# w_in weights as float16 pairs in a hybrid attention and mLSTM layer: one conversion form for all four pieces instead of two forms in turn

## The chip, the cores and the metric

The kernel runs on one core of a Trainium2 chip. The metric is the device time of one execution in microseconds (us). An engine works through its own list of instructions in order and waits for others by semaphores: PE (TensorE) multiplies matrices, ACT (ScalarE) and DVE (VectorE) work element by element, POOL (GpSimd) does a smaller part of that, SP issues most of the transfers between memory (HBM) and the on-chip buffer (SBUF). Products land in PSUM, a small buffer of banks which ACT and DVE read out.

## The reference

One layer of a diffusion backbone over 128 context tokens and 1024 latent tokens, with attention heads and mLSTM heads side by side. Cut to what touches the change:

```python
h = rmsnorm(x, norm1_w) * (1 + sc1) + sh1
aq, ak, av, mq, mk, mv, mo, mg = jnp.split(h @ w_in, SPLIT_POINTS, axis=-1)
...
attn_o = attention(aq, keys, vals)
hm, st_f, st_b = mlstm_bidir(heads(mq), heads(mk) * (MLSTM_DK ** -0.5), heads(mv), gates, init_f, init_b)
hm = rmsnorm(hm...) * jax.nn.sigmoid(mo)
mix = jnp.concatenate([attn_o, hm], axis=-1) @ w_out
x = x + g1 * mix
h2 = rmsnorm(x, norm2_w) * (1 + sc2) + sh2
x = x + g2 * swiglu(h2, w_gu, w_down)
```

D_MODEL is 1024. Of the 2832 columns of w_in, 512 make the queries aq, 256 the keys and values of attention, 16 the gates, and each of the four mLSTM heads has 4 x 128 columns (its mq, mk, mv and mo). The layer norm, the attention, the scans, w_out and the SwiGLU behind them are not changed.

## The kernel before

The 1152 tokens stand as nine blocks of 128 (block 0 is the context, 1 to 8 the latent tokens), in three groups of three. All matrices are float32, and a product with w_in is made from pairs: a weight is scaled by a power of two and split into a float16 "hi" and the float16 rest "lo", the activations h likewise (`hTh`, `hTl`), and three matmuls add hi*hi, hi*lo and lo*hi in PSUM.

The class `Scaled` (from L179) does this for a set of columns of w_in. A set is four pieces `raw` of 128x1024 float32 (1024 rows of w_in are 8 x 128, a piece holds two of the eight and 512 columns). `ready()` takes four `iraw` buffers, loads them (L193), finds the largest absolute value by two ACT passes for each piece (L198) and forms the scale; `pairs()` (L211) makes each piece a pair in an `ipair` buffer; `inverses()` forms the factors that undo the scale. There are four `iraw` and four `ipair` buffers in all. So the load of the next set's piece waits until the pair of the old piece is made (its DVE pass reads `raw` last), and the pair of a next piece waits until PE has used the old pair for the last time.

In the kernel before, `pairs()` has two forms in turn. Pieces 0 and 2 (the even form): ACT multiplies by the scale and rounds to float16 (L218), DVE computes raw*scale - hi (L219). Pieces 1 and 3 (the odd form): ACT multiplies `raw` by the scale in place (L221), ACT copies the result to float16 (L222), DVE subtracts (L137, the line of the helper `sub`). L221 needs only the piece and the scale; L218 and L222 also need the free `ipair` buffer.

Six sets go through it. `kvg` (keys, values, gates) comes first, with 128x544 pieces, and asked for the even form for all four, by `kvg.pairs(1)` at L378. Then come `w_q`, the attention queries (L971), head 0 (L978), and heads 1 to 3 in `head_project` (L746). For the last five sets half of the pieces have the odd form: ten even and ten odd pieces.

In the phase of the heads, `head_project(h)` first computes the transposed queries of all nine blocks, with the pairs as the moving side (`q_group`, L808 to L810), then block after block, 0 to 8, the k, v and o columns (`linear_tok`, L483 to L485); `evac` reads each block's PSUM bank out: `kt` (L755), `va` (L757) and `th` (L760), the last of which frees the bank. Two banks, named `wi`, serve these products. `evac` then transposes kt on PE (L116), copies it (`kT`, L767) and updates the state (L783, L785, `cs` L792 or L796). At the end of a head stands the turn to the next set: PE finishes block 8 with the old pairs, ACT and DVE convert the next set, and PE's next `q_group` needs both a free `wi` bank and the new pairs. Woven in between are the scans of the head before (`head_mlstm`: `dt` L849, `it` L869, `hm` L886, `jkh` L889) and the attention of the blocks: scores S in the only buffer of that name (L1035), their maximum (L1037), the exponential `pr` (L1038, which frees S), and the pair `ph` (L1041) and `pl` (L1042).

The order of each engine's list is not that of the source: a scheduler places the instructions by priorities and by a simulated time of its own for each of them. So a change of one instruction's kind can move the others around it.

Of the kernel before, what the change touches and what calls it, by code (L numbers as in the profile page):

```python
# [13 lines left out]
AF = mybir.ActivationFunctionType  # L14
ALU = mybir.AluOpType
# [30 lines left out]
def hybrid_step(ctx: ExitStack, tc: tile.TileContext, I: dict, O: dict):  # L46
    nc = tc.nc
    mm = nc.tensor.matmul
    act = nc.scalar.activation
    dve = nc.vector  # L50
# [7 lines left out]
    def nm(s):  # L58
        uid[0] += 1
        return f"{s}_{uid[0]}"  # L60
# [10 lines left out]
    def emit(gen):  # L71
        for _ in gen:
            pass
# [62 lines left out]
    def sub(out, full, hi, eng):  # L136
        (dve if eng == "dve" else pool).tensor_tensor(out=out, in0=full, in1=hi, op=ALU.subtract)  # L137
# [41 lines left out]
    class Scaled:  # L179
# [28 lines left out]
            dve.tensor_scalar(out=t[:, 10:11], in0=t[:, 8:9], scalar1=0.5, scalar2=None, op0=ALU.mult)  # L208
            self.inv, self.inv_k, self.inv_half = t[:, 8:9], t[:, 9:10], t[:, 10:11]

        def pairs(self, dve_every=2):  # L211
            out = []
            n, b = self.n, self.shape[1]
            for j, raw in enumerate(self.raws):
                w = wp.tile([P, 2, 1024], F16, name=nm("ipair"), tag="ipair", bufs=4)
                hi, lo = w[:, 0, :n], w[:, 1, :n]
                if j % dve_every == 0:
                    act(hi, raw[:, :n], AF.Copy, scale=self.scale)  # L218
                    dve.scalar_tensor_tensor(out=lo, in0=raw[:, :n], scalar=self.scale, in1=hi, op0=ALU.mult, op1=ALU.subtract)  # L219
                else:  # L220
                    act(raw[:, :n], raw[:, :n], AF.Copy, scale=self.scale)  # L221
                    nc.scalar.copy(hi, raw[:, :n])  # L222
                    sub(lo, raw[:, :n], hi, "dve")
                out.append(tuple(v.rearrange("p (a b) -> p a b", b=b) for v in (hi, lo)))
            return out

# [54 lines left out]
    def rows_of(j):  # L281
        return w_in[2 * j * P : (2 * j + 2) * P, :].rearrange("(a p) n -> p a n", p=P)

    for b in range(2 * CB):
        load_x(b)
    kvg = Scaled([[(lambda v: v[:, :, 0:256], rows_of(j)[:, :, 512:768]),
                   (lambda v: v[:, :, 256:272], rows_of(j)[:, :, 2816:2832])] for j in range(4)], (2, 272),
                 [p0.tile([P, 544], F32, name=f"kraw{j}") for j in range(4)])
# [86 lines left out]
        normalise(c)  # L375
        turn(c)
    emit(kvg_steps)
    kvg_pairs = kvg.pairs(1)  # L378

    for n, out in ((0, shift1), (1, scale1)):  # L380
        halves = [bankA(), bankA()]
# [1166 lines left out]
```

## Time and profile before

| | us |
|---|---|
| time, three runs: median (lowest, highest) | 1572.1 (1570.31, 1574.45) |
| the profiled execution, its own time | 1574.08 |
| its span in the trace | 1572.3 |
| PE busy | 1487.7 |
| DVE busy | 1022.9 |
| ACT busy | 771.8 |
| POOL busy | 271.4 |

The span runs from the first to the last instruction of the trace; some 1.8 us of the execution's own time lie outside it. The granted clock of PE was 0.979 of full speed on average. The five sets of the change are converted between 70 and 375 us; the whole w_in, attention and mLSTM work ends at about 460 us, and from about 580 us on come w_out and the feed-forward part.

### The profile page before, as it was taken

How to read it: one execution, taken by the hardware profiler on the slowest of the kernel's cores; microseconds unless marked ns; L12 is line 12 of the kernel's file. 1: busy time of each engine (PE TensorE's matmuls, PEld its weight loads, DVE VectorE, ACT ScalarE, POOL GpSimd, SP SyncE). 2: the span in 40 equal slices, each digit the busy share in tenths (PEclk: the TensorE clock that was granted, in tenths of full speed). 3: DMA queues.
4: the chain of work that ended last, by engine and by line, in shares of the span. 5: the costliest groups of instructions: out<-in, count | busy, mean ns of one | idle time of the engine just before them, and what ended most of it. 6: DMA issues, size and time to landing. Idle time of an engine off the chain costs nothing.

```text
span 1572.3 us, 23397 instructions
## 1 busy us (share of the span) xinstructions
PE 1487.7 (95%) x8539; PEld 1247.3 (79%) x8539; DVE 1022.9 (65%) x2025; ACT 771.8 (49%) x1409; POOL 271.4 (17%) x357
## 2 busy tenths in 40 slices
PE   6899999999999689999999999999999999999996
PEld 3544567676766468898998989989898989999995
DVE  4878554737659576677555677877866585554555
ACT  4754465847656344545432444556552443323332
POOL 0213333322343242100110101000010101001111
PEclk9899999999999799999999999999999999999998
DMA  9664323523556847767555447878763545544441
GB/s 360 186 182 157 97 68 41 121 47 68 114 150 162 265 80 197 184 174 175 154 154 149 147 126 236 195 170 180 179 162 114 168 133 168 161 130 138 143 139 54
DMA packets 387881, 236.91 MB, mean 151 GB/s; under 512 B 170198, under 2 KB 346790, under 8 KB 387766
## 3 DMA queue, kind: packets, MB, share of 16 engines
q1 hardware_dynamic: 385110, 231.84, 54.1%
q10 hardware_dynamic: 2656, 3.58, 1.1%
q8 instruction: 67, 1.10, 0.3%
q14 instruction: 48, 0.39, 0.1%
HBM read 183.79 MB, written 13.26 MB: 125 GB/s over the span
## 4 chain that ended last, share of the span: by engine, by line
PE 77%; DVE 11%; DMA 5%; ACT 4%; issue 2%; SPq 0%; POOL 0%; ACTq 0%; DVEq 0%; POOLq 0%
PE mm L1316 11%; PE mm L1317 11%; PE mm L1315 11%; PE mm L1115 5%; PE mm L1116 5%; PE mm L1117 5%; PE S L1035 3%; PE wi L483 3%; PE wi L485 3%; PE wi L484 3%; PE mm L116 2%; PE mm L1147 1%; PE mm L1148 1%; PE mm L1149 1%; PE po L1060 1%
## 5 line engine op out<-in xcount | busy, mean ns | idle before, releaser
L152 ACT CAST whi<-raw 128x1024 fp32r<-128x1024 f32 (+1 forms) x216 | 222.3, 1029 | 411.0 <-PE mm L1316 156.5
L137 DVE TENSOR_TENSOR wlo<-raw,whi 128x1024 fp32r<-128x1024 f32 (+1 forms) x216 | 260.4, 1206 | 202.9 <-ACT whi L152 202.3
L1316 PE MATMUL mm<-aTl,whi 128*128 128x384 f32 x1056 | 355.7, 337 | 2.7 <-DVE aTl L137 2.7
L1317 PE MATMUL mm<-aTh,wlo 128*128 128x384 f32 x1056 | 354.3, 336 | 0.0
L1315 PE MATMUL mm<-aTh,whi 128*128 128x384 f32 x1056 | 353.3, 336 | 0.0
L137 POOL TENSOR_TENSOR hl<-tn,hl 128x384 fp32r<-128x384 f32 x66 | 84.4, 1279 | 840.0 <-ACT hl L1338 748.3
L1316 PEld LDWEIGHTS mm<-aTl,whi 128*128 128x128 f32 x1056 | 198.5, 188 | 3.9 <-DVE aTl L137 3.3
L1315 PEld LDWEIGHTS mm<-aTh,whi 128*128 128x128 f32 x1056 | 198.1, 188 | 0.6
L1317 PEld LDWEIGHTS mm<-aTh,wlo 128*128 128x128 f32 x1056 | 198.4, 188 | 0.0
L1116 PE MATMUL mm<-wlo,hl 128*128 128x512 f32 x372 | 145.7, 392 | 0.0
L1115 PE MATMUL mm<-whi,hl 128*128 128x512 f32 x372 | 144.3, 392 | 0.0
L1117 PE MATMUL mm<-whi,hl 128*128 128x512 f32 x372 | 143.4, 392 | 0.0
L483 PE MATMUL wi<-ipair,hT 128*128 128x384 f16 (+2 forms) x408 | 135.6, 335 | 1.7 <-ACT hT L507 1.2
L484 PE MATMUL wi<-ipair,hT 128*128 128x384 f16 (+2 forms) x408 | 135.6, 335 | 0.0
L485 PE MATMUL wi<-ipair,hT 128*128 128x384 f16 (+2 forms) x408 | 132.1, 335 | 1.0 <-DVE hT L137 1.0
L1042 DVE SCALAR_TENSOR_TENSOR pl<-pr,st,ph 128x1152 f16<-128x1152 f32 (+1 forms) x72 | 96.0, 1333 | 31.7 <-ACT ph L1041 31.4
L1037 DVE TENSOR_REDUCE st<-S 128x1 f32<-128x1152 f32 (+1 forms) x72 | 88.9, 1235 | 16.3 <-PE S L1035 16.1
L1038 ACT ACTIVATE pr<-S,st 128x1152 f32<-128x1152 f32 (+1 forms) x72 | 81.3, 1130 | 32.4 <-DVE st L1037 29.3
L1041 ACT ACTIVATE ph<-pr,st 128x1152 f16<-128x1152 f32 (+1 forms) x72 | 83.9, 1165 | 23.8 <-DVE st L1040 6.7
L1035 PE MATMUL S<-kst,qT 128*128 128x384 f32 (+1 forms) x400 | 87.6, 349 | 4.8 <-ACT pr L1038 4.8
L1104 DVE TENSOR_TENSOR t<-mm,gl 128x512 f32<-128x512 f32 x102 | 69.1, 687 | 26.2 <-DMA gl<-g_d 11.5
L1117 PEld LDWEIGHTS mm<-whi,hl 128*128 128x128 f32 x372 | 69.9, 188 | 14.2
(375 smaller groups left out, 2538.4 us busy)
## 6 DMA issues: line engine op xcount, KB each, us to landing
raw<-in_w_gu_dram SPq DMA_DIRECT2D x132, 512.0 KB
raw<-in_w_down_dram SPq DMA_DIRECT2D x60, 512.0 KB
a<-in_w_ada_dram SPq DMA_DIRECT2D x24, 512.0 KB
gl<-g_d SPq DMA_DIRECT2D x36, 256.0 KB
aw<-in_w_ada_dram SPq DMA_DIRECT2D x16, 512.0 KB
iraw<-in_w_in_dram SPq DMA_DIRECT2D x32, 256.0 KB
raw<-in_w_out_dram SPq DMA_DIRECT2D x12, 512.0 KB
x<-in_x_sample_dram SPq DMA_DIRECT2D x11, 512.0 KB
```

Source lines behind the costliest of these rows:

```text
L137: (dve if eng == "dve" else pool).tensor_tensor(out=out, in0=full, in1=hi, op=ALU.subtract)
L152: nc.scalar.copy(hi[:, :n], raw[:, :n])
L483: mm(ps[:, :n], ah, wh[:, k % 2, c0 : c0 + n], start=(k == 0), stop=False)
L484: mm(ps[:, :n], ah, wl[:, k % 2, c0 : c0 + n], start=False, stop=False)
L485: mm(ps[:, :n], al, wh[:, k % 2, c0 : c0 + n], start=False, stop=(k == KD - 1))
L1035: mm(S[:, n, 0:w], qT[:, h, :], kst[kv][:, t, c0 + n * w : c0 + (n + 1) * w], start=(t == 0), stop=(t == 1))
L1115: mm(ps, ah, wh[:, k % 2, :], start=(k == 0), stop=False)
L1116: mm(ps, ah, wl[:, k % 2, :], start=False, stop=False)
L1117: mm(ps, al, wh[:, k % 2, :], start=False, stop=(k == nk - 1))
L1315: mm(ps, wh[:, k, :], th[:, k, :], start=(k == 0), stop=False)
L1316: mm(ps, wh[:, k, :], tl[:, k, :], start=False, stop=False)
L1317: mm(ps, wl[:, k, :], th[:, k, :], start=False, stop=(k == KD - 1))
```

## The change

`pairs()` loses its two forms. Every piece takes the even form: one ACT pass from the float32 piece to the scaled float16 hi, and one DVE instruction for raw*scale - hi. For `kvg` nothing changes, since it had asked for that already. Behind the class every line number of the changed kernel is 5 lower than in the kernel before; in the class L218 is now L217 and L219 is L218.

```diff
--- before.py
+++ after.py
@@ -208,19 +208,14 @@
             dve.tensor_scalar(out=t[:, 10:11], in0=t[:, 8:9], scalar1=0.5, scalar2=None, op0=ALU.mult)
             self.inv, self.inv_k, self.inv_half = t[:, 8:9], t[:, 9:10], t[:, 10:11]
 
-        def pairs(self, dve_every=2):
+        def pairs(self):
             out = []
             n, b = self.n, self.shape[1]
-            for j, raw in enumerate(self.raws):
+            for raw in self.raws:
                 w = wp.tile([P, 2, 1024], F16, name=nm("ipair"), tag="ipair", bufs=4)
                 hi, lo = w[:, 0, :n], w[:, 1, :n]
-                if j % dve_every == 0:
-                    act(hi, raw[:, :n], AF.Copy, scale=self.scale)
-                    dve.scalar_tensor_tensor(out=lo, in0=raw[:, :n], scalar=self.scale, in1=hi, op0=ALU.mult, op1=ALU.subtract)
-                else:
-                    act(raw[:, :n], raw[:, :n], AF.Copy, scale=self.scale)
-                    nc.scalar.copy(hi, raw[:, :n])
-                    sub(lo, raw[:, :n], hi, "dve")
+                act(hi, raw[:, :n], AF.Copy, scale=self.scale)
+                dve.scalar_tensor_tensor(out=lo, in0=raw[:, :n], scalar=self.scale, in1=hi, op0=ALU.mult, op1=ALU.subtract)
                 out.append(tuple(v.rearrange("p (a b) -> p a b", b=b) for v in (hi, lo)))
             return out
 
@@ -375,7 +370,7 @@
         normalise(c)
         turn(c)
     emit(kvg_steps)
-    kvg_pairs = kvg.pairs(1)
+    kvg_pairs = kvg.pairs()
 
     for n, out in ((0, shift1), (1, scale1)):
         halves = [bankA(), bankA()]
```

ACT's list is shorter by ten instructions, those of L221; the lists of the other engines keep their length but for waits. On each engine the order of the instructions differs in places up to the end of the heads, and is the same after it. The places that the prediction speaks of:

PE at the turn from head 1 to head 2. The rows are S (scores), wi_3524 (block 8 of head 1, its first and its last matmul; it is wi_3518 in the change) and, at the end, the first query product of head 2 with the new pairs (L808, now L803). Before:

```order
L1035 MATMUL S_3730<-kst_1027,qT_2949 128x384 x6
L846 MATMUL mm_3322<-NM_105,selb 128x256
L116 MATMUL mm_3341<-ident,kt_3331 128x128
L1035 MATMUL S_3800<-kst_1027,qT_2949 128x384 x6
L785 MATMUL mm_3348<-wv_3345,kt_3331 128x258
L483 MATMUL wi_3524<-ipair_2604,hT_441 128x384
...
L485 MATMUL wi_3524<-ipair_2614,hT_441 128x384
L1035 MATMUL S_3992<-kst_1027,qT_2949 128x384 x6
L116 MATMUL mm_3429<-ident,kt_3419 128x128
L866 MATMUL mm_3475<-c_253_1944,qT_2055 128x129
L808 MATMUL wi_3654<-hT_439,ipair_3619 128x384
```

And with the change:

```order
L1030 MATMUL S_3722<-kst_1027,qT_2943 128x384 x6
L841 MATMUL mm_3316<-NM_105,selb 128x256
L478 MATMUL wi_3518<-ipair_2600,hT_441 128x384
...
L480 MATMUL wi_3518<-ipair_2609,hT_441 128x384
L1030 MATMUL S_3792<-kst_1027,qT_2943 128x384 x6
L116 MATMUL mm_3423<-ident,kt_3413 128x128
L861 MATMUL mm_3469<-c_253_1940,qT_2051 128x129
L868 MATMUL mm_3481<-va_2581,sd_3323 128x129 x2
L1030 MATMUL S_3984<-kst_1027,qT_2943 128x384 x6
L803 MATMUL wi_3646<-hT_439,ipair_3613 128x384
```

The second S moves from ahead of block 8 to behind it, and the third S, with one scan product, from well ahead of the query products to right in front of them.

ACT at the same turn, from about the first conversion of head 2's set (iraw_2621 to 2624 before, iraw_2615 to 2618 now) to `th` of block 7, the one that frees the bank for the query products. Before:

```order
L755 ACTIVATE kt_3501<-wi_3442,isc_2076 128x128
L218 ACTIVATE ipair_3619<-iraw_2621,isc_2872 128x1024
L1038 ACTIVATE pr_3796,st_3799<-S_3800,st_3799 128x1152
L796 COPY cs_3352<-mm_3348 128x129
L222 COPY ipair_3622<-iraw_2622 128x1024
L889 ACTIVATE jkh_3312,ssh_2657<-hm_2656 128x128
L869 ACTIVATE it_3385<-mm_3382,QT 128x129 x2
L757 ACTIVATE va_3503<-wi_3442,isc_2076 128x128
L218 ACTIVATE ipair_3626<-iraw_2623,isc_2872 128x1024
L1041 ACTIVATE ph_3797<-pr_3796,st_3799 128x1152
L222 COPY ipair_3629<-iraw_2624 128x1024
L760 ACTIVATE th_3506<-wi_3442,isc_2076 128x128
```

And with the change, where `hm`, `cs`, `jkh`, `it` (two) and one `kT`, six small instructions, stand between these rows too:

```order
L217 ACTIVATE ipair_3613<-iraw_2615,isc_2866 128x1024
L1033 ACTIVATE pr_3718,st_3721<-S_3722,st_3721 128x1152
L217 ACTIVATE ipair_3616<-iraw_2616,isc_2866 128x1024
L762 COPY kT_3337<-mm_3335 128x128
L750 ACTIVATE kt_3495<-wi_3436,isc_2072 128x128
L217 ACTIVATE ipair_3619<-iraw_2617,isc_2866 128x1024
L1036 ACTIVATE ph_3719<-pr_3718,st_3721 128x1152
L217 ACTIVATE ipair_3622<-iraw_2618,isc_2866 128x1024
L198 ACTIVATE jkw,isc_3903<-iraw_3628 128x512
L752 ACTIVATE va_3497<-wi_3436,isc_2072 128x128
L1033 ACTIVATE pr_3788,st_3791<-S_3792,st_3791 128x1152
L755 ACTIVATE th_3500<-wi_3436,isc_2072 128x128
```

One exponential more (pr_3718 and pr_3788 where there was pr_3796 alone), and one |max| pass over the next set's first piece (L198), stand between the first conversion and `th`. The two L221 of this set, which stood 18 rows ahead of its first conversion, are gone.

DVE at the turn from w_q to head 0: `ipair_1892` to `ipair_1899` (now 1890 to 1896) are the set's pieces 0 to 2, `qraw` the attention queries after their rotation, QT a table of the mLSTM gates that the first products of head 0 wait for. Before:

```order
L679 TENSOR_TENSOR nr_213_1629<-qraw_1606,ss_1036 128x16x16 x2
L219 TENSOR_SCALAR ipair_1892<-iraw_1059,isc_1211,ipair_1892 128x1024
L686 TENSOR_TENSOR qraw_1606<-qraw_1606,nr_213_1629 128x512
L137 TENSOR_TENSOR ipair_1895<-iraw_1060,ipair_1895 128x1024
L666 TENSOR_REDUCE nrs_1759<-nr_224_1757 128x16
L219 TENSOR_SCALAR ipair_1899<-iraw_1061,isc_1211,ipair_1899 128x1024
L333 TENSOR_TENSOR shift_90<-mm_1823,bcol 128x8
L654 COPY QT<-mm_1841 128x512
```

And with the change:

```order
L674 TENSOR_TENSOR nr_213_1627<-qraw_1604,ss_1036 128x16x16 x2
L681 TENSOR_TENSOR qraw_1604<-qraw_1604,nr_213_1627 128x512
L218 TENSOR_SCALAR ipair_1890<-iraw_1057,isc_1209,ipair_1890 128x1024
L661 TENSOR_REDUCE nrs_1757<-nr_224_1755 128x16
L218 TENSOR_SCALAR ipair_1893<-iraw_1058,isc_1209,ipair_1893 128x1024
L218 TENSOR_SCALAR ipair_1896<-iraw_1059,isc_1209,ipair_1896 128x1024
L328 TENSOR_TENSOR shift_90<-mm_1821,bcol 128x8
L649 COPY QT<-mm_1839 128x512
```

Piece 0's instruction moves behind that of qraw, and piece 1's behind a sum (L666, now L661); QT stands behind piece 2 as it did. (The small steps of a square root between them are left out of both.)

## The prediction

> **What bounds the kernel now.** I read the page's totals first, then PE's waits, then windows and the timeline at the five turns from one set of weights to the next: A into w_q, B into head 0, C, D and E into heads 1, 2 and 3. From the page, the busy time of each engine and the chain of waits that ended last:
>
> ```profile
> PE 1487.7 (95%) x8539; PEld 1247.3 (79%) x8539; DVE 1022.9 (65%) x2025; ACT 771.8 (49%) x1409; POOL 271.4 (17%) x357
> ...
> PE 77%; DVE 11%; DMA 5%; ACT 4%; issue 2%; SPq 0%; POOL 0%; ACTq 0%; DVEq 0%; POOLq 0%
> ```
>
> PE is busy 95% of the span; ACT, which loses work here, 49%, and 4% of the chain lies on it. ACT time counts only where PE stands and waits for it. The list of PE's waits (what for: total us, times, longest) has these rows from the phase of the heads:
>
> ```profile
> PE S L1035 <- ACT pr L1038: 4.8, 4, 2.1
> ...
> PE wi L808 <- ACT th L760: 2.1, 1, 2.1
> ...
> PE wi L808 <- DVE QT L654: 2.0, 1, 2.0
> ...
> PE mm L866 <- ACT kT L767: 0.6, 1, 0.6
> ```
>
> No row of the list names a conversion (ipair) as what PE waited for. But `th`, `pr`, `kT` and QT stand in the lists of ACT and DVE among the conversions, and move with them. The windows of turns B, C and D (from:to, length, busy time of PE, PEld, DVE, ACT, POOL, granted clock, DMA share, GB/s):
>
> ```profile
> 152.00:170.00 18.00, 16.02 (x86) 8.22 (x84) 13.16 (x27) 11.94 (x22) 3.17 (x2) 0.91 0.46 134
> 216.00:230.00 14.00, 14.00 (x92) 9.37 (x91) 9.17 (x20) 13.12 (x38) 5.22 (x8) 1.00 0.54 144
> 276.00:310.00 34.00, 30.27 (x186) 22.37 (x184) 26.06 (x68) 32.06 (x79) 9.65 (x21) 0.95 0.52 120
> ```
>
> At C, PE never stops. At B it stops for 2.0 us with ACT busy two thirds of the time. At D ACT is busy for 32.06 of 34 us: the one turn where ACT sets the pace, and the only one where shorter ACT work can pay directly.
>
> **The change part by part.** The groups of the conversion (count: shortest/median/longest ns, first to last start):
>
> ```profile
> L221 ACT ACTIVATE iraw<-iraw,isc x10: 1135/1144/1154, 70.2 to 357.7; 128x1024 f32<-128x1024 f32 x10
> ...
> L218 ACT ACTIVATE ipair<-iraw,isc x10: 1134/1152/1183, 85.0 to 369.6; 128x1024 f16<-128x1024 f32 x10
> L222 ACT CAST ipair<-iraw x10: 1032/1049/1105, 87.1 to 372.1; 128x1024 f16<-128x1024 f32 x10
> L219 DVE SCALAR_TENSOR_TENSOR ipair<-iraw,isc,ipair x10: 1279/1284/1520, 87.2 to 372.9; 128x1024 f16<-128x1024 f32 x10
> L137 DVE TENSOR_TENSOR ipair<-iraw,ipair x10: 1212/1224/2695, 89.3 to 374.9; 128x1024 f16<-128x1024 f32 x10
> ```
>
> Removed: ten L221, 10 x 1.144 = 11.4 us of ACT. Changed: ten ACT copies become L218, 10 x (1.152 - 1.049) = +1.0 us; ten subtractions become L219, 10 x (1.284 - 1.224) = +0.6 us of DVE. Net -10.4 us of ACT, all of it off PE's path unless a turn says otherwise: the two L221 of a set need only the piece and its scale, and run well ahead of the turn (the first at 70.2 us, where the first L218 runs at 85.0). They are hidden by ACT's own idle time. What comes after the old pair is free stays four ACT passes and four DVE instructions. If that cover is gone, as at D, two of them cost 2 x 1.144 = 2.3 us.
>
> **Turns A, C, E.** At A and C PE stops for nothing, and a set's two odd pieces are 0.10 us longer on ACT and 0.06 on DVE: I take +0.1 at A, 0 at C (bounds: -0.3, nothing to gain there; +3.7 for a new stop, priced with the rivals). At E PE stops 0.6 us for `kT`, behind an odd piece's copy that grows by 0.1: +0.2 (bounds -0.6, the wait gone, to +2).
>
> **Turn B.** Timeline (start, us, engine, line; in brackets the idle time before it and what ended it):
>
> ```profile
> 152.95 1.27 POOL L685 TENSOR_TENSOR qraw<-qraw,cc 128x512 f32<-128x512 f32 x1 [1.22 <-DVE nr L679]
> 154.09 1.29 DVE L219 SCALAR_TENSOR_TENSOR ipair<-iraw,isc,ipair 128x1024 f16<-128x1024 f32 x1 [1.28 <-ACT ipair L218]
> 155.29 0.69 DVE L686 TENSOR_TENSOR qraw<-qraw,nr 128x512 f32<-128x512 f32 x1
> 155.41 1.07 SPq L193 DMA_DIRECT2D iraw<-in_w_in_dram  x2
> 157.88 6.71 SPq L193 DMA_DIRECT2D iraw<-in_w_in_dram  x4
> 159.81 0.63 ACT L198 ACTIVATE jkw<-iraw 128x512 bf16<-128x512 f32 x1 [1.77 <-DMA iraw<-in_w_in_dram]
> 164.28 0.69 DVE L654 COPY QT<-mm 128x512 f32<-128x512 f32 x1
> 165.01 0.32 PE L808 MATMUL wi<-hT,ipair 128*128 128x384 f16 x1 [1.98 <-DVE QT L654]
> ```
>
> It is one chain: piece 0's pass on DVE (ends 155.38) frees `raw`; SP issues the next set's load (155.41); ACT, idle for 1.77 us, waits for it with the |max| pass at 159.81; behind that stand piece 2's ACT and DVE passes, then QT, then PE. In the changed order of DVE piece 0's pass comes behind the one for qraw (L686), which needs POOL's product (there at 152.95 + 1.27 = 154.2) and so starts about then. The pass then ends 0.9 us later, and every step of the chain with it: **+0.9** (bounds: 0, if the scheduler's order lets QT run as early as before; +2.1 = 0.9 and the 1.2 of the L666 sum, now ahead of piece 1's pass, if that delays the second load too).
>
> **Turn D.** First the ACT rows that are gone, then what leads to the query products:
>
> ```profile
> 276.57 2.18 ACT L221 ACTIVATE iraw<-iraw,isc 128x1024 f32<-128x1024 f32 x2
> ...
> 283.68 1.24 ACT L1038 ACTIVATE pr<-S,st 128x1152 f32<-128x1152 f32 x1
> 285.07 2.11 PE L1035 MATMUL S<-kst,qT 128*128 128x384 f32 x6 [1.13 <-ACT pr L1038]
> 287.22 1.36 DVE L1037 TENSOR_REDUCE st<-S 128x1 f32<-128x1152 f32 x1 [0.97 <-PE S L1035]
> 288.76 0.33 PE L483 MATMUL wi<-ipair,hT 128*128 128x384 f16 x1
> 288.92 0.33 PE L484 MATMUL wi<-ipair,hT 128*128 128x384 f16 x1
> 289.45 1.15 ACT L218 ACTIVATE ipair<-iraw,isc 128x1024 f16<-128x1024 f32 x1 [1.00 <-PE wi L485]
> 290.50 1.20 ACT L1038 ACTIVATE pr<-S,st 128x1152 f32<-128x1152 f32 x1
> 293.86 1.16 ACT L218 ACTIVATE ipair<-iraw,isc 128x1024 f16<-128x1024 f32 x1
> 294.90 1.26 ACT L1041 ACTIVATE ph<-pr,st 128x1152 f16<-128x1152 f32 x1
> 296.05 1.05 ACT L222 CAST ipair<-iraw 128x1024 f16<-128x1024 f32 x1
> 296.98 0.38 ACT L760 ACTIVATE th<-wi,isc 128x128 f32<-128x128 f32 x1
> 297.39 0.66 ACT L198 ACTIVATE jkw<-iraw 128x512 bf16<-128x512 f32 x1
> 297.42 0.32 PE L808 MATMUL wi<-hT,ipair 128*128 128x384 f16 x1 [2.14 <-ACT th L760]
> ```
>
> Here PE stops twice: 1.13 us for `pr`, since the second S needs the only score buffer, and 2.14 us for `th`. In the changed order block 8 comes ahead of the second S, so the first stop goes and block 8 starts near 283.9 instead of 287.8. Its first conversion (289.45 now, released by PE) can then run from about 285.2. From there I add ACT's starts, from one row to the next: a conversion 1.05, `pr` 1.20, `ph` 1.15, a |max| pass 0.65, the small ones 0.15 to 0.5. Four conversions 4.2, two `pr` 2.4, `ph` 1.15, |max| 0.65, nine small ones 2.7: 11.1 in all, where it is 296.98 - 289.45 = 7.5 now; the last `pr` starts at about 294.9, `th` near 296.1 (now 296.98). But the third S now stands directly ahead of the query products and waits for that last `pr`; from its end, 296.1, PE needs some 1.1 us for S (six matmuls; 2.11 above, at half the clock), so the queries start near 297.2, against 297.42, and PE has done 0.4 more beside (the scan product that moved ahead): -0.6. The stop does not go, it joins: PE's work ahead of the third S (24 matmuls of block 8, 0.16 apart as at 288.76 and 288.92, 3.9; S 1.1; scans and transposes 3.4) ends near 292.5, so one stop of some 3.5 us stands where there were two of 3.3.
>
> After stops PE also runs at half the granted clock (windows as above):
>
> ```profile
> 166.00:168.00 2.00, 2.00 (x8) 0.88 (x6) 2.00 (x1) 1.00 (x4) 1.28 (x1) 0.50 0.52 153
> 286.00:287.00 1.00, 1.00 (x5) 1.00 (x5) 0.25 (x1) 1.00 (x2) 0.01 (x1) 0.50 1.11 207
> 374.00:376.00 2.00, 2.00 (x9) 0.95 (x8) 2.00 (x4) 1.82 (x5) 0.66 (x1) 0.51 0.60 122
> ```
>
> Such a stretch lasts about 3.4 us (by the row widths of matmuls around it) and so costs 1.7 us of PE. Three of the four stops (B, D's first, E) brought one; the 2.14 us before 297.42 did not (that matmul took its usual 0.32). In the first stop of D it was off the path, since ACT came last there; behind the joined stop it is on it, at a chance near one: +1.6. **D: -0.6 + 1.6 = +1.0** (bounds: -5.0, both stops and the half clock gone, 1.13 + 2.14 + 1.7; +4.6, below).
>
> [...]
>
> **The sum.** 0.1 + 0.9 + 0 + 1.0 + 0.2 = +2.2 on the profiled execution's 1574.08: 1576.3. That execution is 2.0 above the median of 1572.1, so 1574.3 as a median. Behind the heads (from about 460 us) orders are the same and everything shifts.
>
> **The rivals.**
>
> *Rival 1, ACT's relief reaches PE (faster).* If at D `pr` and `th` come as early as ACT's list allows, 2.3 us less work in a stretch at 94%, and the stop shrinks below what halves the clock, D gives -5.0 instead of +1.0; with the rest +1.2 that is -3.8, and if E's stop and half clock go too (0.6 + 1.7, its own +0.2 with them) -6.3. Time 1565.8 to 1568.3. For it: ACT's 32.06 of 34. Against it: the third S stands behind the last `pr` by order, and `pr` behind four conversions.
>
> *Rival 2, a load in ACT's list ahead of th (slower).* In the changed order the |max| pass of the next set's first piece stands ahead of `va`, the last `pr` and `th` of D; now it stands behind them (297.39). Its load can start only when piece 0's DVE pass has freed `raw`. At B the load was there 159.81 - 155.38 = 4.4 us after that; queue rows like 157.88 show four transfers taking 6.71. ACT reaches the pass at about 293.5. With DVE's pass done at 287.6 at the earliest, it waits for nothing up to 5.9 us; if a maximum (1.36) and a `pl` (1.4) come first on DVE, the pass ends at 290.3, and with 6.7 us ACT stands until 297.0, 3.5 late, with `pr`, `th` and PE behind it: D = -0.6 + 3.5 + 1.7 = +4.6, in all +5.8: 1577.9. It decides from a pass that ends later than 293.5 - 4.4 = 289.1. For it: the 1.77 us that ACT stood for just this load at B. Against it: DVE had 8 of 34 us idle there.
>
> *Rival 3, a new stop at a turn that has none (slower).* If at C, where ACT is busy 13.12 of 14 us, the slightly longer conversions and their new order bring a stop like those of B and D, it costs 2.0 and the half clock 1.7: +3.7, in all +5.9, 1578.0. Against it: only conversions of 1.05 that become 1.15 there, and PE has other work.
>
> *That it does nothing* is inside the forecast: the removed work was hidden, 0 to +1.
>
> **How the numbers follow.** 0.3% of the time, 4.7 us, is about what a measurement of this kernel can tell from no change. The forecast has a chance of 0.42 (0.36 within, 0.06 slower by more), rival 1 has 0.24 (0.20 faster, 0.04 within), rival 2 has 0.22 (0.20 slower, 0.02 within), rival 3 has 0.12, all slower. So faster 0.20, same 0.42, slower 0.38. The forecast's own range is 1571 to 1577. For 8 in 10 I go down to 1564 (rival 1 and a little of B's stop, 2.0) and up to 1584 (rivals 2 and 3 together, +9.5, are 1581.6, and the +1.2 and +1.8 that B and E reach by their bounds).
>
> **What would show it.** Right: no L221 rows; ACT busy near 771.8 - 10.4 = 761; queries of the fourth set at D within 1 us of 297.4 plus B's shift, with one PE stop of about 3.5 us for `pr` in front of the S ahead of them, and 0.50 clock behind it; at B piece 0's DVE pass behind qraw's and the QT stop near 2.9 us. Wrong: D's stops gone (rival 1); ACT idle for a DMA at the |max| pass ahead of `th` (rival 2); PE stopping around 216 to 225 us (rival 3); or any shift of more than 1 us that appears after 460 us, where I expect none.

## The result and the profile after

The changed kernel takes 1578.46 us in the median of 6 runs (1576.19 to 1580.49), the kernel before 1571.6 in 6 runs. The ratio is 1.0039, with a 95% interval of 1.0029 to 1.0049: slower by some 6 us. Forecast were +2.2 us and a median of 1574.3; the measured time lies in the stated range, beyond the forecast's own one of 1571 to 1577. All ratios here and below compare fast executions only, and leave two far outliers out (1890.7 us of the kernel before, 3832.77 us in the last run).

The profiled execution took 1580.49 us, with a span of 1578.7. First its totals and the groups of the conversion (count: shortest/median/longest ns, first to last start):

```profile
PE 1489.9 (94%) x8539; PEld 1246.3 (79%) x8539; DVE 1023.7 (65%) x2025; ACT 759.7 (48%) x1399; POOL 271.7 (17%) x357
```

```profile
L217 ACT ACTIVATE ipair<-iraw,isc x20: 1132/1149/1204, 85.7 to 378.6; 128x1024 f16<-128x1024 f32 x20
L218 DVE SCALAR_TENSOR_TENSOR ipair<-iraw,isc,ipair x20: 1272/1283/1582, 86.9 to 381.4; 128x1024 f16<-128x1024 f32 x20
```

The change did what it says: twenty passes of one form, no L221, and 12.1 us less ACT work (771.8 - 759.7, where 10.4 were worked out). The time went the other way. What PE waits for shows where (what for: total us, times, longest):

```profile
PE S L1030 <- ACT pr L1033: 4.1, 3, 2.1
...
PE wi L803 <- DVE QT L649: 2.8, 1, 2.8
PE mm L780 <- ACT it L864: 2.8, 1, 2.8
...
PE mm L868 <- DVE sd L846: 1.4, 1, 1.4
```

The wait for QT at turn B grew from 2.0 to 2.8 us, that for `th` at turn D (2.1) has become one for `it` (2.8), and a wait for `sd` of 1.4 us is new. Turn B in the timeline of the changed kernel, the same chain as before:

```profile
157.44 0.69 DVE L681 TENSOR_TENSOR qraw<-qraw,nr 128x512 f32<-128x512 f32 x1 [1.45 <-POOL qraw L680]
...
158.05 1.28 DVE L218 SCALAR_TENSOR_TENSOR ipair<-iraw,isc,ipair 128x1024 f16<-128x1024 f32 x1
...
163.72 0.63 ACT L198 ACTIVATE jkw<-iraw 128x512 bf16<-128x512 f32 x1 [2.93 <-DMA iraw<-in_w_in_dram]
...
166.33 1.29 DVE L218 SCALAR_TENSOR_TENSOR ipair<-iraw,isc,ipair 128x1024 f16<-128x1024 f32 x1 [2.84 <-ACT ipair L217]
...
168.11 0.68 DVE L649 COPY QT<-mm 128x512 f32<-128x512 f32 x1
...
168.84 0.32 PE L803 MATMUL wi<-hT,ipair 128*128 128x384 f16 x1 [2.77 <-DVE QT L649]
```

The whole execution is 3.0 us late when it gets here (ACT's pass on piece 0 starts at 155.94, before at 152.91). Without those 3.0, piece 0's pass on DVE starts at 155.05 instead of 154.09, behind qraw's; the |max| pass at 160.7 instead of 159.81, QT at 165.1 instead of 164.28, and PE goes on at 165.84 instead of 165.01: the chain is 0.8 to 1.0 us later from end to end, as the prediction's step said. Turn D:

```profile
289.64 1.15 ACT L217 ACTIVATE ipair<-iraw,isc 128x1024 f16<-128x1024 f32 x1 [0.35 <-PE wi L480]
...
296.26 1.15 ACT L217 ACTIVATE ipair<-iraw,isc 128x1024 f16<-128x1024 f32 x1
...
297.30 0.62 ACT L864 ACTIVATE it<-mm,QT 128x129 f32<-128x129 f32 x2
...
297.80 0.64 ACT L198 ACTIVATE jkw<-iraw 128x512 bf16<-128x512 f32 x1
...
298.07 0.67 PE L780 MATMUL mm<-wv,kt 128*128 128x258 f32 x2 [2.76 <-ACT it L864]
...
298.81 1.26 ACT L1033 ACTIVATE pr<-S,st 128x1152 f32<-128x1152 f32 x1
...
300.02 0.40 ACT L755 ACTIVATE th<-wi,isc 128x128 f32<-128x128 f32 x1
...
301.38 2.27 PE L1030 MATMUL S<-kst,qT 128*128 128x384 f32 x6
...
303.45 0.54 PE L803 MATMUL wi<-hT,ipair 128*128 128x384 f16 x1
```

The two stops have joined, as forecast, but not where: PE stands 2.76 us for `it`, which ACT's list has behind all four conversions (the fourth starts at 296.26). When the third S comes up (301.38), `pr` has been done for 1.3 us. The matmul of 0.54 us instead of 0.32 shows the half clock (granted there: 0.50, for 6.83 us from 299.36 on).

One place is to be added to what was said of the order: three PE instructions near 1290 us also stand in another order. No shift of lasting size is seen there.

### The profile page after: what moved, and what is told of

It reads as the page before. It is cut to its first block, busy times and chain, and to the rows that moved or that the text cites. A ratio compares the mean times of both kernels' runs of the same rounds, so it can differ in the third digit from the quotient of the medians.

```text
span 1578.7 us, 23387 instructions
## 1 busy us (share of the span) xinstructions
PE 1489.9 (94%) x8539; PEld 1246.3 (79%) x8539; DVE 1023.7 (65%) x2025; ACT 759.7 (48%) x1399; POOL 271.7 (17%) x357
## 5 line engine op out<-in xcount | busy, mean ns | idle before, releaser
L137 POOL TENSOR_TENSOR hl<-tn,hl 128x384 fp32r<-128x384 f32 x66 | 85.1, 1290 | 841.2 <-ACT hl L1333 721.1
```

## The experiments

The order of each engine's list can be fixed, apart from the instructions themselves. The scheduler keeps to an edge between two instructions of one engine that asks for their order and for no wait. Before the schedule is made, such edges are drawn along a table of each engine's list; the code of the edit is the same in all the runs below that have one, and only the table differs.

```diff
+def pin(tc):
+    made = [i for i in tc.nc.cur_bb.bb.instructions if type(i).__name__ != "BassTilePoolBoundary" and i.name not in EXTRA]
...
+    for engine, row in zip(("PE", "DVE", "Activation", "Pool", "SP"), rows):
+        mine = [i for i in made if str(i.engine).rsplit(".", 1)[-1] == engine]
...
+            if prev is not None:
+                tc.add_manual_dep(mine[k], prev.name, info, reason="pin")
...
     with tile.TileContext(nc, **TC_OPTS) as tc:
+        del EXTRA[:]
         hybrid_step(tc, ins, outs)
+        pin(tc)
```

(`EXTRA` holds the L221, which only one of the two kernels has, so they keep no fixed place.) This separates two theories: that the time follows the order in which the scheduler put things, or the instructions that the change put in.

**The two crossings.** The changed kernel with the table of the order before:

> The changed instructions (one ACT pass and one multiply-and-subtract for every piece, no L221), with every engine's list held in the order of the kernel before. Theory 'order' (the 6.9 us come from where the scheduler put things): within 2 us of before, and a little below it, since 10.4 us of ACT work are gone and nothing is moved; turn B stops PE 2.0 us as before. Theory 'instructions' (the longer conversions and DVE passes cost it themselves): 1577 to 1580, as the changed kernel.

And the kernel before (with its L221) with the table of the changed order:

> The instructions of the kernel before (two forms in turn, ten L221), with every engine's list held in the order of the changed kernel; the L221 are placed by the scheduler. Theory 'order': 1576 to 1581, the stop at B near 2.8 us, a joined stop at D. Theory 'instructions': within 2 us of before.

| instructions | order | ratio to before (95%) | median us |
|---|---|---|---|
| changed | before | 1.000 (0.999 to 1.001) | 1571.1 |
| before | changed | 1.0046 (1.0029 to 1.0063) | 1578.4 |
| changed | changed | 1.0039 (1.0029 to 1.0049) | 1578.46 |

The totals of the first, in the profile:

```profile
PE 1486.4 (94%) x8539; PEld 1245.6 (79%) x8539; DVE 1020.8 (65%) x2025; ACT 760.5 (48%) x1399; POOL 270.6 (17%) x357
```

It has the changed kernel's 760 us of ACT work and the time of the kernel before; the second has the 770 us and the loss. So the loss is the order's. The changed instructions alone are worth nothing, within 0.1%; in the changed order the instructions of either kernel bring the loss, with intervals that overlap.

**Both kernels again**, for a second profile each:

> The kernel before once more, for a second profile: which stops of PE and which half-clock stretches come again. If the stretches at 135, 166, 285 and 374 us come again and none at 84 or 118, they belong to the program; if others come, part of the 6.4 us between the two profiles is chance of one execution.

> The changed kernel once more, for a second profile. If the half-clock stretches at 84 and 118 us and the stop at 116 us come again, the 3.0 us that the changed kernel is late before turn B belong to the program; if not, they are chance, and the mean loss has to come from B (0.8) and from the heads (some 2 us).

They took 1569.01 and 1580.23 us. In the kernel before, none of the half-clock stretches at 166, 285 and 374 us came again, only the one at 134. In the changed kernel those near 82, 170 and 300 us did, the one at 118 not. So single stretches came and went from one execution to the next, and what a turn costs has to be read over many executions.

**Turn by turn.** The changed instructions in the order before, but for a part of the lists with the changed order: up to about 146 us (A), 146 to 195 (B), 195 to 255 (C), 255 to 330 (D).

> The changed instructions in the order of the kernel before, except that up to about 146 us (turn A and the conditioning products around it) every list has the order of the changed kernel. Theory 'order at A brings a half-clock stretch near 83 us': +2 to +3.5 us, with such a stretch in the profile. The prediction's own step (+0.1 at A): within 1 us of before.

> The same, with the changed kernel's order only from about 146 to 195 us (turn B). The prediction's step: +0.9, the stop for QT near 2.7 us where it is 1.5 to 2.0. Rival: the moved DVE pass costs nothing by itself, 0.

> The same, with the changed kernel's order only from about 195 to 255 us (turn C and the scans after it). The prediction's step: 0. Theory 'new stop' (its third rival, but at 234 us, where PE waits for sd): +1 to +1.5.

> The same, with the changed kernel's order only from about 255 to 330 us (turn D). The prediction's step: +1.0, one joined stop and a half-clock stretch behind it. Its second rival (a load in ACT's list): +4.6, with ACT idle for a DMA at the |max| pass. Theory 'half clock alone': +1.7, the stops together as long as before.

| changed order at | ratio (95%) | us (ratio less 1, times 1572) |
|---|---|---|
| A alone | 0.9998 (0.9989 to 1.0007) | -0.3 (-1.7 to 1.1) |
| B alone | 1.0003 (0.9993 to 1.0013) | 0.5 (-1.1 to 2.0) |
| C alone | 1.0013 (1.0002 to 1.0024) | 2.0 (0.3 to 3.8) |
| D alone | 1.0009 (0.9999 to 1.0019) | 1.4 (-0.2 to 3.0) |

At A the theory of a half-clock stretch fell (none near 83 us in its profile, and no loss), and the prediction's own step held. Of the others only C is clear of no change by itself. The profiles say more than these times, since each effect comes back in its place. For B alone, the wait for QT and the window from 160 to 176 us (the last three numbers are the granted clock, the DMA share and GB/s):

```profile
PE wi L803 <- DVE QT L649: 3.3, 1, 3.3
```

```profile
160.00:176.00 16.00, 12.69 (x71) 7.58 (x69) 9.28 (x26) 9.84 (x22) 4.26 (x2) 0.89 0.55 160
```

and the same two of the changed instructions in the order before (the first crossing):

```profile
PE wi L803 <- DVE QT L649: 1.5, 1, 1.5
```

```profile
160.00:176.00 16.00, 13.96 (x91) 9.00 (x90) 11.06 (x22) 9.89 (x21) 4.26 (x2) 1.00 0.44 134
```

A clock of 0.89 over 16 us is one stretch of 3.4 us at half clock (0.5 x 3.4 / 16 = 0.11). For C alone, the timeline of PE's new stop, with the first query product of head 1 ahead of it:

```profile
219.36 0.33 PE L803 MATMUL wi<-hT,ipair 128*128 128x384 f16 x1
...
225.40 0.63 ACT L198 ACTIVATE jkw<-iraw 128x512 bf16<-128x512 f32 x1 [1.23 <-DMA iraw<-in_w_in_dram]
...
227.49 0.63 ACT L198 ACTIVATE jkw<-iraw 128x512 bf16<-128x512 f32 x1 [0.55 <-DMA iraw<-in_w_in_dram]
...
228.26 1.15 ACT L844 ACTIVATE dt<-mm,QT 128x128 f32<-128x128 f32 x4
...
229.06 0.42 DVE L846 TENSOR_TENSOR sd<-mm,dt 128x256 f32<-128x256 f32 x1
...
229.53 0.71 PE L868 MATMUL mm<-va,sd 128*128 128x129 f32 x4 [0.78 <-DVE sd L846]
```

and the same place in the first crossing:

```profile
218.17 0.33 PE L803 MATMUL wi<-hT,ipair 128*128 128x384 f16 x1
...
227.00 0.63 ACT L198 ACTIVATE jkw<-iraw 128x512 bf16<-128x512 f32 x1 [0.61 <-DMA iraw<-in_w_in_dram]
...
227.63 1.12 ACT L844 ACTIVATE dt<-mm,QT 128x128 f32<-128x128 f32 x4
...
228.27 0.42 DVE L846 TENSOR_TENSOR sd<-mm,dt 128x256 f32<-128x256 f32 x1 [0.54 <-ACT dt L844]
...
230.34 0.61 PE L868 MATMUL mm<-va,sd 128*128 128x129 f32 x4
```

PE waits for `sd`, that for `dt`, and `dt` stands behind |max| passes that wait for their load. But that is so in the order before too, and counted from the first query product `dt` comes no later: 8.9 us behind it at C alone, 9.5 in the order before. What moved is PE: it comes to this scan product (L868) 9.4 us behind its first query product (229.53 - 0.78 - 219.36), where it was 12.2, since 18 query products that stood ahead of the scan product now stand behind it.

For D alone, the wait and the window of the turn:

```profile
PE mm L780 <- ACT it L864: 2.8, 1, 2.8
```

```profile
284.00:308.00 24.00, 20.21 (x119) 15.05 (x118) 19.55 (x46) 21.62 (x57) 7.71 (x15) 0.93 0.56 123
```

0.93 is one stretch at half clock (0.07 of 24 us); the first crossing had 1.00 in this window.

**The halves, and all but A**, with the changed kernel itself on the chip of the halves:

> The changed instructions, the changed kernel's order on every list up to about 195 us (turns A and B), the order of the kernel before from there on. If the parts add up as measured alone (A 0, B +0.5): 1571 to 1573. Theory 'A and B feed each other' (the three profiles of the full new order, 4.3 us late when head 0 begins): +3 to +5.

> The changed instructions, the order of the kernel before up to about 195 us, the changed kernel's order from there on (turns C, D, E). If the parts add up (C +2.0, D +1.4, E unknown): +3 to +4. If the loss sits in A and B: +1 to +2. Rival, that turn E holds the rest: +6 to +7.

> The changed kernel itself on the same chip as the two halves: +5 to +8 as before, for the sum of the halves to be held against.

> The changed instructions in the changed kernel's order from about 146 us on (turns B to E), in the order of the kernel before up to there. The halves summed to +2.5 us where the whole loses 5 to 7. If A counts only together with the rest (its late chain and half-clock stretch in front of turn B): +1.5 to +3. If A counts for nothing and B feeds the turns behind it: +5 to +7.

| changed order | ratio (95%) | us |
|---|---|---|
| up to 195 us (A, B) | 1.0006 (0.9996 to 1.0017) | 0.9 (-0.6 to 2.7) |
| from 195 us on (C, D, E) | 1.0010 (0.9999 to 1.0022) | 1.6 (-0.2 to 3.5) |
| all (the changed kernel) | 1.0032 (1.0020 to 1.0044) | 5.0 (3.1 to 6.9) |
| from 146 us on (B to E) | 1.0034 (1.0021 to 1.0047) | 5.3 (3.3 to 7.4) |

Without A's order the loss is still whole: A is not needed for it, and the half-clock stretch near 83 us, which three of the six profiles with the changed order there had, came in one of the eight with the order before as well. The waits of the last run are those of the changed kernel:

```profile
PE wi L803 <- DVE QT L649: 3.0, 1, 3.0
...
PE mm L780 <- ACT it L864: 2.8, 1, 2.8
...
PE mm L868 <- DVE sd L846: 1.5, 1, 1.5
```

The halves' medians add up to 2.5 us, the whole is 5.0 on the same chip; with these intervals (each about 1.8 us to either side) that is not a contradiction, and no proof that the turns feed each other either.

**What the profiles add up to.** There are 14 profiles in all, and at each of the turns B, C and D seven have the order before and seven the changed one:

| at the turn | order before | changed order |
|---|---|---|
| B: from ACT's pass on piece 0 to its DVE pass, mean us | 1.2 | 2.1 |
| B: from the same to the maximum pass, and to QT, mean us | 6.3, 10.9 | 7.8, 12.2 |
| B: stop for QT, mean (range) us | 1.5 (1.1 to 2.0) | 2.8 (2.6 to 3.3) |
| B: clock of the window 0.89 (one stretch) | in 1 of 7 | in 7 of 7 |
| C: stop for `sd` near 228 to 236 us | none | 1.1 (0.7 to 1.5) |
| D: stops together, mean us | 3.5 | 3.6 |
| D: half-clock stretches in the window | 3 in 7 | 10 in 7 |

A stretch of 3.41 us at a granted clock of 0.50 costs PE half of that, 1.7 us, by estimate, where PE is not late for another reason. B: 1.3 of stop and 6/7 x 1.7 = 1.5 of clock, less a stop of 0.4 for the query copy `qT` that goes, 2.4. C: 1.1. D: 1.7 of clock, with stops as long as before. Together 5.2 us, beside 5.0 to 7.2 measured for the whole in three comparisons. This sum is an estimate from 14 executions; the timed runs confirm its sign at C and its total, not each part.

The same profiles allow a check without any price for a stretch, by the start of each head's first query product (L803; L808 in the kernel before):

| stretch of time, mean (range) us | order before | changed order |
|---|---|---|
| ACT's pass on head 0's piece 0 to head 0's first query product (B) | 11.6 (11.2 to 12.1) | 13.0 (12.7 to 13.4) |
| head 0's to head 1's (the clock behind B) | 54.3 (54.0 to 55.1) | 55.3 (55.0 to 55.4) |
| head 1's to head 3's (C and D, both or neither changed) | 152.6 (152.1 to 153.9) | 155.0 (153.5 to 156.5) |
| head 3's to the end | 1198.1 (1194.9 to 1203.2) | 1197.4 (1195.9 to 1199.9) |

That is 1.4, 1.0 and 2.4, together 4.8 us, and nothing behind head 3's first query product. Between 400 and 470 us PE's stops differ in kind but add up to as much (3.7 to 3.9 us with the changed order, 3.0 to 4.6 with the order before).

No version that beats both came of it: the changed instructions in the old order are as fast as the kernel before, and not faster.

## Why the prediction was right or wrong

**That the removed ACT work is hidden** was right, and is shown: taking 10 us of ACT work away in an unchanged order moves the time by 0.0% (within 0.1), and putting it back into the changed order takes nothing of the loss away. Rival 1 (ACT's relief reaches PE) is refuted for the order that the scheduler chose, and at the old order too: there D's stops keep 3.5 us, with two passes fewer on ACT in front of them.

**Turn A, +0.1.** Measured -0.3 (-1.7 to 1.1), as forecast. The first profile alone would have misled: it was 3.0 us late by turn B, by stretches at 84 and 118 us; the first came in half of the profiles with this order and in one of eight without, the second in this profile alone, and the timed runs of A show no loss.

**Turn B, +0.9.** The mechanism was right: piece 0's DVE pass comes 0.9 us later behind ACT's in all seven profiles of the changed order, and the load, the |max| pass, piece 2 and QT later with it. Over seven profiles of each order QT is 1.4 later, not 0.9, since the load lands later still. The size was wrong for another reason. The prediction took the half-clock stretch behind this stop for a property of the kernel before, since its one profile had it; in 7 profiles of that order it came once, and behind the longer stop 7 times in 7. That is 1.5 us more, by the table above. The timed run of B alone (0.5, -1.1 to 2.0) is below the 2.4, the one of A and B together (0.9, -0.6 to 2.7) allows it; how much of B's loss reaches the end when it stands alone is left open.

**Turn C, 0.** Wrong: this is the step that failed. "At A and C PE stops for nothing" was read from the turn itself, and the new stop stands 10 us behind it, among the scans. Rival 3 had priced a stop at C (3.7, with half clock), but gave the longer conversions as its cause. The cause is PE's own list: a scan product comes up 2.8 us earlier than before, and what it needs from ACT and DVE does not. Measured +2.0 (0.3 to 3.8) for C alone; 1.1 us of stop in the profiles, with no half clock behind it (granted 1.00 from 222 to 240 us in all seven).

**Turn D, +1.0.** The sign and about the size held: measured +1.4 (-0.2 to 3.0), and one stop in the main in place of two, with half clock behind it in all seven profiles (granted 0.86 to 0.93 over 284 to 308 us). ACT's part came out: first conversion to `th` takes 10.4 us (289.64 to 300.02; forecast 11.1, 7.5 before). PE's part did not. The prediction let PE go through the scans and transposes to the third S without a wait (-0.6), and stop there for `pr`. But a product that stands ahead of the third S (L780) waits for `it`, which is behind the four conversions too, so PE stopped there, and S and the queries came later: the first query product starts at 303.45, where 297.42 and the 3.8 us of lateness at B's end make 301.2. So the queries were 2.2 us late, where the prediction's own sign of being right allowed 1; C's stop is 1.4 of them. The +1.6 of half clock is what the measured loss consists of. It was also wrong to take the stretch at D of the profile before for free: the two profiles of the kernel before differ by 1.6 us from head 1's to head 2's first query product (77.3 with that stretch, 75.7 without). Rival 2 did not come here: the |max| pass at 297.80 waits for no DMA.

**Turn E, +0.2.** Its stops are as before (1.1 and 0.7; 1.0 and 0.6 in the kernel before); no run had E alone, and the stretch from head 3's first query product to the end shows no loss.

**The chances.** The forecast's case was "within 0.3%" at 0.42, slower had 0.38; the ratio of 1.0039 lies just beyond. The sum's mis-sized terms are C (0 for 1.1), the clock at B (0 for 1.5) and D (1.0 for 1.7); with the first two alone +2.2 becomes 4.8. That 1578.46 lies inside the stated range is in part luck: the part of it above 1577 was there for rivals 2 and 3, of which the one did not come and the other came smaller, later and by another cause.

## What to carry to other kernels

A change that takes hidden work away can still cost time, because a scheduler that places instructions by their simulated times will move others: judge such a change by the order it leaves on the bottleneck's own list and on those of the engines that hold it up, and test it by giving the new instructions the old order and the old ones the new order. Look for new stops behind the place of the change too, where the bottleneck comes to something earlier than what it needs. One profile does not tell what a stop costs when the clock may halve behind it, as it did behind the stop for `th`, 2.1 to 2.2 us long, in two of seven profiles; compare the same place in several.

## What the runs showed of the hardware

In the profile of the kernel before, six stretches of PE at a granted clock of 0.50 begin between 64 and 460 us, at 70.26, 135.11, 165.83, 285.30, 374.05 and 459.38 us, and each lasts 3.41 us. In the first profile of the changed kernel five of 3.41 us begin there, at 70.67, 84.32, 118.45, 138.93 and 169.65 us, and one of 6.83 us at 299.36, which counts as two in the table of the turns.

The stop for `th` at D in the order before is 2.1 to 2.2 us long in all seven profiles, and brought a stretch in two, so here its length alone did not decide it. One of each, in three windows of time around the stop (length, busy time of PE, granted clock, DMA share, GB/s), first from the run with C alone, then from the kernel before:

```profile
292.85:296.27 3.42, 1.25 (x9) 1.00 0.85 236
296.27:299.68 3.41, 3.41 (x13) 0.50 0.66 174
299.68:303.09 3.41, 3.41 (x23) 1.00 0.45 134
```

```profile
292.12:295.53 3.41, 3.15 (x20) 1.00 0.57 162
295.53:298.95 3.42, 1.53 (x10) 1.00 0.68 182
298.95:302.36 3.41, 3.41 (x24) 1.00 0.84 241
```

At B the stops of 1.1 to 1.6 us brought no stretch in six profiles, the one of 2.0 us in the kernel before brought one, and those of 2.6 to 3.3 us did in all seven; 7 in 7 need not hold for every execution. What decides whether a stretch follows a stop is open.
